# Three quarters of the last down projection as seven half-size block products, with the next quarter's up projection between them

## The chip, the cores and the metric

The kernel runs on one core of one Trainium2 chip, as one program. The time is device microseconds of that core, the median of three runs. A core has TensorE (PE in the rows: matmuls, and PEld: the loads of their stationary operand), VectorE (DVE), ScalarE (ACT), GpSimd (POOL) and SyncE (SP, which issues most of the DMAs). Each engine works through its own instructions in order and waits on semaphores of the others.

## What is computed

A two-layer decoder trunk over 512 tokens of width 1024, all in float32: differential attention and an MLP, then multi-head latent attention and an MLP, then a norm. The change is in the second MLP and in what follows it:

```python
def sq_relu_mlp(hn, w_up, w_down):
    return jnp.square(jax.nn.relu(hn @ w_up)) @ w_down
...
        h = h + sq_relu_mlp(rms_norm(h, mlp_norm_g[l]), w_up[l], w_down[l])
    return rms_norm(h, final_norm_g)
```

Here `hn` is 512 x 1024, `w_up` 1024 x 4096 and `w_down` 4096 x 1024.

## The kernel before

**Three matmuls for one.** Every operand is split into a high part (a cast to the type fp32r, on ScalarE) and a low part (what the cast left over, a subtraction on VectorE). `mm3` multiplies high by high, high by low and low by high, so a float32 product of 128 x 128 by 128 x 512 is three matmuls. Lines 346, 347 and 348 are these three.

**Weights.** The class `Weights` (object `W`) holds a list of units of 128 x 1024 elements in the order in which they are used. A unit is loaded by SP into one of four raw buffers, then cast (L101, `...h`) and subtracted (L113, `...l`) into one of three buffer pairs (`DEPTH`). `W.get` hands out the next unit, `W.ahead` prepares those behind it: as far as one unit ahead. A unit can't be cast before the matmuls of the unit three places earlier have read its buffer.

**The last MLP.** It goes in two halves of the 4096 hidden features. `hidden` makes the up projection: weights stationary, the normed tokens (`xn0`, `xn1`, high and low) moving, two banks of 128 features x 512 tokens at a time from a unit `m1u_0` (inputs 0 to 511) and a unit `m1u_4` (512 to 1023). Each finished bank gets a Relu on ScalarE (L676), a product with itself on VectorE (L677) and a split into high and low (L332, L333), 16 tiles in a half. The first four of these tile pairs go into `krest`, eight 128 x 512 tiles at the low end of SBUF that earlier stages used for attention keys, the others into tiles of the pool `big` (`m1hh`, `m1hl`). `down_tokens` makes the down projection: hidden features stationary (128 features x 128 tokens), weights moving (`m1d_0` to `m1d_14`, eight units of two times 128 features x 512 outputs), four banks of 128 tokens x 512 outputs, once for each half `fc` of the outputs. `token_done` scales a bank by the token's norm factor `r2c` and adds it to the residual tile `rt` on VectorE; behind the second half it also starts the final norm.

A unit is thus 24 matmuls with 512 columns, up or down. The last MLP has 32 units up (16 in each half) and 32 down.

**Beside the first up projection** runs `scale1`: it sums the squares of the stream over features by matmuls (`m1csps`, from `ssq_m`, which GpSimd has added up), makes `r2c`, and turns the residual `res` into token rows by 8 groups of transposes (`rT`), each copied by ScalarE into a tile `rt`. `side` calls the next step of it whenever so many microseconds of matmuls, by the program's own reckoning, have been issued: 4.0.

Nothing but these lists, the buffers and the order in which the code asks for things sets the order; a scheduler in the framework may move instructions of one engine a few places.

Of the kernel before, what the change touches and what calls it, by code (L numbers as in the profile page):

```python
# [15 lines left out]
P = 128  # L16
# [43 lines left out]
class Weights:  # L60
# [5 lines left out]
    def __init__(self, nc, pool, size):  # L66
        self.nc, self.pool, self.size = nc, pool, size
        self.specs, self.raws, self.parts = [], [], []
        self.taken = self.split = 0
        self.eng = nc.vector  # L70
# [13 lines left out]
    def load(self, upto, queue=None):  # L84
        while len(self.raws) < min(upto, len(self.specs)):
            name, shape, loads, *_ = self.specs[len(self.raws)]
            raw = self.tile(F32, name + "r", "raw", shape, self.RAW)
            for to, src in loads:
                (queue or self.nc.sync).dma_start(raw[to], src)
            self.raws.append(raw)  # L90

    def prep_h(self, upto):

        while len(self.parts) < min(upto, len(self.specs)):
            n = len(self.parts)
            self.load(n + 1)
            name, shape, _, beside, outs, eng = self.specs[n]
            h = self.tile(F32R, name + "h", "wh", (P, shape[1], shape[2] * (2 if beside else 1)), self.DEPTH)
            l = h if beside else self.tile(F32R, name + "l", "wl", shape, self.DEPTH)
            for d, v in outs or [(lambda t: t[:, :, :shape[2]], lambda t: t)]:  # L100
                self.nc.scalar.copy(d(h), v(self.raws[n]))  # L101
            self.parts.append((h, l))

    def prep(self, upto):

        self.prep_h(upto)
        while self.split < min(upto, len(self.specs)):
            n = self.split
            name, shape, _, beside, outs, eng = self.specs[n]
# [6 lines left out]
            self.load(n + 1 + self.RAW)  # L116

    def get(self, n):
        assert n == self.taken, (n, self.taken, self.specs[n][0])
# [3 lines left out]
        return got  # L123

    def ahead(self):
        self.prep(self.taken + 1)


class Filler:
# [132 lines left out]
def trunk(ctx: ExitStack, tc: tile.TileContext, io: dict, out: bass.AP):  # L262
# [17 lines left out]
    def bank(name, tag):  # L280
        return ps.tile([P, T], F32, name=name, tag=tag, bufs=BANKS[tag])
# [14 lines left out]
    def w_unit(w, c0, n, k0, nk, name, **kw):  # L296
        return W.add(name, (P, nk, n), [((ALL,), w_view(w, c0, n, k0, nk))], **kw)
# [42 lines left out]
        split_into(h, l, src, scale)  # L340
        return h, l

    def mm3(dst, a, b, start, stop):

        (ah, al), (bh, bl) = a, b
        nc.tensor.matmul(dst, ah, bh, start=start, stop=False)  # L346
        nc.tensor.matmul(dst, ah, bl, start=False, stop=False)  # L347
        nc.tensor.matmul(dst, al, bh, start=False, stop=stop)  # L348
        us = 3 * PASS * max(256, dst.shape[-1])
        later.spent(us)  # L350
        return us
# [451 lines left out]
    last_b = [out_proj(w_ob, heads_b, 4, 4, split_for(xs_m1, G_MLP_B, ssq_m1), "ob", OP_TAGS)]  # L803


    hid1 = [[], []]
# [6 lines left out]
    def down_tokens(w_dn, hid, half, fc, last):  # L813

        units = [(w_unit(w_dn, fc * T, T, 16 * half + k, 2, f"m1d{half}{fc}_{k}"), k) for k in range(0, 16, 2)]
        tags = ("s", "s", "tr", "tr") if (half + fc) % 2 else ("acc", "acc", "acc", "o")
        late = 2 if last else 0

        def job():
            dsts = [bank(f"m1d{half}{fc}{i}", t) for i, t in enumerate(tags)]  # L820

            def mul(i, w, k):
                for kk in range(2):
                    yield mm3(dsts[i], sub(hid[k + kk], ALL, slice(i * P, (i + 1) * P)), sub(w, ALL, kk),
                              k + kk == 0, k + kk == 15)

            for u, k in units[:8 - late]:
                w = W.get(u)
                for i in range(NT):
                    yield from mul(i, w, k)  # L830
                    if i == 1:
                        W.ahead()
                    if k == 14:
                        token_done(i, dsts[i], half, fc)
            ws = [(W.get(u), k) for u, k in units[8 - late:]]
            for i in range(NT if late else 0):
                for w, k in ws:
                    yield from mul(i, w, k)
                token_done(i, dsts[i], half, fc)
        return 16 * NT * 3 * PASS * T, job  # L840

    def token_done(i, dst, half, fc):
        t = rtok[i][fc]
        nc.vector.scalar_tensor_tensor(t, dst, r2c[:, i:i + 1], t, op0=ALU.mult, op1=ALU.add)
        if half == 0:
            return
        junk = big("fjunk")
        nc.scalar.activation(junk, t, AF.Square, accum_out=fss[:, i, fc:fc + 1])
        if fc == 0:
            nc.gpsimd.tensor_mul(t, t, gfin[0][:, :T])  # L850
            nc.vector.tensor_scalar(fss[:, i, 0:1], fss[:, i, 0:1], 1.0 / D, EPS, op0=ALU.mult, op1=ALU.add)
            return
        e, f = small("fe", 1), fr[:, i:i + 1]
        nc.vector.tensor_scalar(e, fss[:, i, 1:2], 1.0 / D, fss[:, i, 0:1], op0=ALU.mult, op1=ALU.add)
        nc.gpsimd.tensor_tensor(f, e, mhalf, op=ALU.pow)

        def out_first():
            o0 = rtok[i][0]
            nc.scalar.activation(o0, o0, AF.Copy, scale=f)
            nc.scalar.dma_start(out_d[i][:, :T], o0)  # L860

        def out_second():
            nc.vector.scalar_tensor_tensor(t, t, f, gfin[0][:, T:], op0=ALU.mult, op1=ALU.mult)
# [4 lines left out]
    up1, down1 = [None, None], [None, None]  # L868
    for half in range(2):
        up1[half] = hidden(io["w_up"][1], xs_m1, half, hid1[half], "m1")  # L870
        down1[half] = [down_tokens(io["w_down"][1], hid1[half], half, fc, half == 1 and fc == 1) for fc in range(2)]


    x_d = io["x"].rearrange("o (i p) d -> (o i) p d", p=P)
# [290 lines left out]
```

## Time and profile before

| | |
|---|---|
| median of 3 runs | 1147.07 us (1147.04 to 1147.47) |
| the profiled execution's own time | 1147.38 us |
| its span, first to last instruction | 1145.6 us |
| TensorE busy | 98% of the span |
| VectorE busy | 57% |
| ScalarE busy | 43% |
| last MLP (start of the first up matmul, of the last down matmul) | 781.46, 1135.72 us |

A row of the timeline has the start in us, the duration, the engine, the line, what it writes and reads, and in brackets how long the engine was idle before it and what ended that. Buffer numbers are left out of names. The duration of a matmul contains its way through the array, so that neighbours overlap; the distance between the starts of two neighbours is what one of them costs. The same holds, less strongly, for VectorE and ScalarE: the next instruction starts somewhat before the end of the one ahead.

### The profile page before, as it was taken

What the parts mean: (1) busy time and instruction counts of PE and PEld (TensorE: products, weight loads), DVE (VectorE), ACT (ScalarE), POOL (GpSimd) and SP (SyncE); (2) the same over time, 40 slices, a digit from 0 to 9 for tenths busy, and PEclk for the clock granted to TensorE, in tenths of its full rate; (3) what the DMA queues carried; (4) which work ended last, traced back from release to release, by engine and by line L of the source; (5) the groups of instructions that cost most, each with busy time, mean ns of one, the idle gap of its engine ahead of it and who ended that gap; (6) DMA issues with size and microseconds to landing.
All of it is one profiled execution on the core that took longest, in us unless ns stands there. A gap on an engine that the chain in (4) does not pass through costs nothing.

```text
span 1145.6 us, 14137 instructions
## 1 busy us (share of the span) xinstructions
PE 1125.5 (98%) x5528; PEld 945.5 (83%) x5528; DVE 649.5 (57%) x1148; ACT 496.9 (43%) x910; POOL 70.6 (6%) x63
## 2 busy tenths in 40 slices
PE   7999999999999999999999999999999999999996
PEld 7778998878888888888888889988888888888885
DVE  5898989876443234444455898855444223444232
ACT  6567666654341213443334666534433112343132
POOL 1000000030000010000111000013000000000011
PEclk9999999999999999999999999999999999999998
DMA  7321222123233333332332220123322333333211
GB/s 230 103 71 56 74 75 75 55 74 111 92 94 108 93 92 93 108 94 92 93 100 80 78 74 19 56 92 92 92 92 92 99 103 92 92 101 101 92 55 74
DMA packets 98321, 102.06 MB, mean 89 GB/s; under 512 B 4896, under 2 KB 86478, under 8 KB 98254
## 3 DMA queue, kind: packets, MB, share of 16 engines
q1 hardware_dynamic: 96974, 99.51, 28.2%
q10 hardware_dynamic: 1280, 1.65, 0.4%
q8 instruction: 43, 0.70, 0.2%
q14 instruction: 24, 0.20, 0.1%
HBM read 99.05 MB, written 2.10 MB: 88 GB/s over the span
## 4 chain that ended last, share of the span: by engine, by line
PE 79%; DVE 12%; ACT 4%; issue 2%; DMA 1%; SPq 1%; POOL 1%; ACTq 0%; POOLq 0%; DVEq 0%
PE m0d L346 5%; PE m1u L346 5%; PE m0d L348 5%; PE m1u L348 5%; PE m0u L347 5%; PE m0u L346 5%; PE m0d L347 5%; PE m1u L347 5%; PE m0u L348 5%; PE m1d L347 4%; PE m1d L348 4%; PE m1d L346 4%; PE m1d L51 3%; PE ob L346 1%; PE ob L348 1%
## 5 line engine op out<-in xcount | busy, mean ns | idle before, releaser
L346 PE MATMUL m1u<-xn1h,m1u_4h 128*128 128x512 f32 x128 | 50.3, 393 | 0.0
L346 PE MATMUL m1u<-xn0h,m1u_0h 128*128 128x512 f32 x128 | 50.2, 392 | 0.0
L348 PE MATMUL m1u<-xn1h,m1u_4l 128*128 128x512 f32 x128 | 49.9, 390 | 0.0
L348 PE MATMUL m1u<-xn0h,m1u_0l 128*128 128x512 f32 x128 | 49.9, 390 | 0.0
L347 PE MATMUL m1u<-xn1l,m1u_4h 128*128 128x512 f32 x128 | 49.8, 389 | 0.0
L347 PE MATMUL m1u<-xn0l,m1u_0h 128*128 128x512 f32 x128 | 49.8, 389 | 0.0
L347 PE MATMUL m0u<-xm0l,m0u_0h 128*128 128x512 f32 x128 | 49.8, 389 | 0.0
L346 PE MATMUL m0u<-xm0h,m0u_0h 128*128 128x512 f32 x128 | 49.8, 389 | 0.0
L346 PE MATMUL m0u<-xm1h,m0u_4h 128*128 128x512 f32 x128 | 49.8, 389 | 0.0
L347 PE MATMUL m0u<-xm1l,m0u_4h 128*128 128x512 f32 x128 | 49.8, 389 | 0.0
L348 PE MATMUL m0u<-xm0h,m0u_0l 128*128 128x512 f32 x128 | 49.8, 389 | 0.0
L348 PE MATMUL m0u<-xm1h,m0u_4l 128*128 128x512 f32 x128 | 49.8, 389 | 0.0
L113 DVE TENSOR_TENSOR m1u_4l<-m1u_4r,m1u_4h 128x1024 fp32r<-128x1024 f32 x16 | 19.6, 1225 | 36.5 <-ACT m1u_4h L101 36.5
L113 DVE TENSOR_TENSOR m0u_4l<-m0u_4r,m0u_4h 128x1024 fp32r<-128x1024 f32 x16 | 19.9, 1245 | 33.4 <-ACT m0u_4h L101 33.2
L677 DVE TENSOR_TENSOR m1a<-m1u,m1a 128x512 f32<-128x512 f32 x32 | 22.0, 687 | 21.7 <-ACT m1a L676 21.7
L677 DVE TENSOR_TENSOR m0a<-m0u,m0a 128x512 f32<-128x512 f32 x32 | 21.9, 686 | 19.4 <-ACT m0a L676 19.4
L101 ACT CAST m1u_4h<-m1u_4r 128x1024 fp32r<-128x1024 f32 x16 | 16.8, 1052 | 34.7 <-PE m1u L347 21.6
L676 ACT ACTIVATE m0a<-m0u 128x512 f32<-128x512 f32 x32 | 18.9, 592 | 29.4 <-PE m0u L348 29.4
L676 ACT ACTIVATE m1a<-m1u 128x512 f32<-128x512 f32 x32 | 19.0, 592 | 27.6 <-PE m1u L348 27.6
L101 ACT CAST m0u_4h<-m0u_4r 128x1024 fp32r<-128x1024 f32 x16 | 16.8, 1052 | 31.7 <-PE m0u L347 25.5
L363 POOL TENSOR_TENSOR ssq_m<-ssq_m,sq 128x512 f32<-128x512 f32 x14 | 21.3, 1519 | 149.8 <-ACT sq L362 149.7
L113 DVE TENSOR_TENSOR m0u_0l<-m0u_0r,m0u_0h 128x1024 fp32r<-128x1024 f32 x16 | 21.0, 1310 | 14.7 <-ACT m0u_0h L101 14.4
(2306 smaller groups left out, 3522.9 us busy)
## 6 DMA issues: line engine op xcount, KB each, us to landing
m0u_0r<-in_w_up SPq DMA_DIRECT2D x16, 512.0 KB, 3.7
m0u_4r<-in_w_up SPq DMA_DIRECT2D x16, 512.0 KB, 3.6
m1u_0r<-in_w_up SPq DMA_DIRECT2D x16, 512.0 KB, 3.6
m1u_4r<-in_w_up SPq DMA_DIRECT2D x16, 512.0 KB, 3.7
wq_0r<-in_w_qkv_a SPq DMA_DIRECT2D x8, 512.0 KB, 3.9
wk_0r<-in_w_qkv_a SPq DMA_DIRECT2D x8, 512.0 KB, 5.0
xt<-in_x SPq DMA_DIRECT2D x8, 256.0 KB, 4.8
wv_0r<-in_w_qkv_a SPq DMA_DIRECT2D x4, 512.0 KB, 3.5
```

What stands on the lines that cost most here:

```text
L51: return self.owner.tc.keep_in_program_order(op(*args, **kw))
L101: self.nc.scalar.copy(d(h), v(self.raws[n]))
L113: eng.tensor_sub(d(to), v(self.raws[n]), d(h).bitcast(F32))
L346: nc.tensor.matmul(dst, ah, bh, start=start, stop=False)
L347: nc.tensor.matmul(dst, ah, bl, start=False, stop=False)
L348: nc.tensor.matmul(dst, al, bh, start=False, stop=stop)
L363: eng(nc).tensor_add(accum, accum, sq)
L676: nc.scalar.activation(a, dst, AF.Relu)
L677: nc.vector.tensor_mul(a, dst, a)
```

## The change

The first three quarters of the hidden features (1024 each, a chunk) get their down projection in another form, the last quarter keeps `down_tokens`. In a chunk the hidden activations A (512 tokens x 1024 features) and the weights B (1024 features x 1024 outputs) are cut in two both ways; A11 is the first 256 tokens and 512 features, B12 the first 512 features and the last 512 outputs. Instead of eight block products there are seven, of blocks and of sums and differences of blocks (S1 to S4 of A, T1 to T4 of B; Winograd's form of Strassen's scheme), and the sums over products are made in three PSUM chains (`u`, `v`, `w`) whose running values are added to `rt` at seven points. A product is 24 matmuls of 512 columns (two units of 12), an eighth of the chunk's old 192.

The hidden activation is now squared by ScalarE (L881 of the new kernel, two pieces of 128 x 256) and kept in float32; the seven left operands are split when they are needed, all into `krest` tiles (a pair of tile pairs per product, in turn). The weights of a chunk are loaded whole: the left column into tiles that attention had used, the right column into `res`, once `scale1` has read it. Weight units may now be such blocks or sums, so `load`, `prep_h` and `prep` skip or call them, and `W.lead = 2` prepares two units ahead while the chunks run. The up projection goes by quarters and by units (`hidden_half`): the first quarter ahead of everything, then one unit of the next quarter behind each product, and one more at a chunk's end. `side` is called with 2.0 in place of 4.0, the norm's weights are two tiles in place of one.

```diff
+            k, ahead = n + 1, 0
+            while k < len(self.specs) and ahead < self.RAW:
+                ahead += not callable(self.specs[k][2])
+                k += 1
+            self.load(k)
...
-        self.prep(self.taken + 1)
+        self.prep(self.taken + self.lead)
...
+        ORDER = (("A11", "B11", "u", [(0, 0)]), ("A12", "B21", "v", [(0, 0)]), ("S2", "T2", "u", [(0, 1)]),
+                 ("S1", "T1", "w", [(1, 1)]), ("S3", "T3", "u", [(1, 1)]), ("S4", "B22", "w", [(0, 1)]),
+                 ("A22", "T4", "u", [(1, 0)]))
...
+        def hidden_tile(self, n, a):
+            k, u, j = n // 4, n % 4 // 2, n % 2
+            for m in range(2):
+                name = f"A{m + 1}{k + 1}"
+                if j == 0:
+                    self.a.setdefault(name, []).append(big(f"m1{name}{self.at}{u}").rearrange("p (k q) -> p k q", k=2))
+                nc.scalar.activation(self.a[name][u][:, j, :], a[:, m * 256:(m + 1) * 256], AF.Square)
...
+        def sum_a(self, to, x, y, op, place=None):
+            x, y = self.a[x], self.a[y]
+            t = self.a[place] if place else [big(f"m1{to}{self.at}{u}").rearrange("p (k q) -> p k q", k=2) for u in range(2)]
+            for u in range(2):
+                nc.vector.tensor_tensor(t[u], x[u], y[u], op)
+            self.a[to] = t
+
+        def sum_b(self, to, x, y, place=None):
+            x, y = self.b[x], self.b[y]
+            t = self.b[place] if place else [[big(f"m1{to}{self.at}{u}{j}") for j in range(2)] for u in range(2)]
+            for u in range(2):
+                if isinstance(t[u], list) or isinstance(x[u], list) or isinstance(y[u], list):
+                    for j in range(2):
+                        nc.vector.tensor_sub(*(v[u][j] if isinstance(v[u], list) else v[u][:, j, :] for v in (t, x, y)))
+                else:
+                    nc.vector.tensor_sub(t[u], x[u], y[u])
+            self.b[to] = t
+
+        def pair(self, name):
+            spare = key_rests[2 * (Sevenths.made % 2):][:2]
+            Sevenths.made += 1
+            self.pairs[name] = [split(a.rearrange("p k q -> p (k q)"), name, tiles=spare[u])
+                                for u, a in enumerate(self.a[name])]
...
+        def product(self, i, units):
+            a, b, chain, to = self.ORDER[i]
+            first = chain not in self.banks
+            if first:
+                self.banks[chain] = [bank(f"m1{chain}{self.at}{t}", "s" if chain == "u" else "tr") for t in range(2)]
+            for u in range(2):
+                w = W.get(units[u])
+                for t in range(2):
+                    for j in range(2):
+                        tok = slice(j * 256 + t * P, j * 256 + (t + 1) * P)
+                        yield mm3(self.banks[chain][t], sub(self.pairs[a][u], ALL, tok), sub(w, ALL, j),
+                                  first and u == j == 0, u == j == 1, skip_group_check=True)
+                        if t == j == 0:
+                            W.ahead()
+                    if u == 1:
+                        for m, n in to:
+                            x = rtok[2 * m + t][n]
+                            tok = 2 * m + t
+                            nc.vector.scalar_tensor_tensor(x, self.banks[chain][t], r2c[:, tok:tok + 1], x,
+                                                           op0=ALU.mult, op1=ALU.add)
...
+        steps = {
+            ("P", 0): lambda: (s.pair("A12"), s.sum_b("T1", "B12", "B11"), s.sum_a("S1", "A21", "A22", ALU.add)),
+            ("U", 0): lambda: (s.sum_b("T2", "B22", "T1"), load("B11")),
+            ("P", 1): lambda: (s.sum_a("S2", "S1", "A11", ALU.subtract), s.pair("S2")),
+            ("U", 1): lambda: s.sum_b("T3", "B22", "B12", "B12"),
+            ("P", 2): lambda: (s.pair("S1"), s.sum_a("S4", "A12", "S2", ALU.subtract, "A12")),
+            ("U", 2): lambda: (s.sum_b("T4", "B21", "T2", "T2"), load("B21")),
+            ("P", 3): lambda: (s.sum_a("S3", "A11", "A21", ALU.subtract, "A21"), s.pair("S3")),
+            ("P", 4): lambda: s.pair("S4"),
+            ("P", 5): lambda: (s.pair("A22"), load("B12")),
+            ("P", 6): lambda: (load("B22"), nxt is not None and nxt.pair("A11")),
+        }
+
+        def with_step(name, gen):
+            for at, us in enumerate(gen):
+                yield us
+                if at == 0 and name in steps:
+                    steps[name]()
+
+        def job():
+            for i in range(7):
+                yield from with_step(("P", i), s.product(i, plan[i]))
+                yield from with_step(("U", i), halves[i]())
+            yield from halves[7]()
+        return (7 * 8 + 8 * 16 / 2) * 3 * PASS * T, job
...
-    side(up1[0], scale1(), 4.0)
-    gfin.append(ap.tile([P, D], F32, name="gfin", tag="atl", bufs=2))
-    nc.sync.dma_start(gfin[0], io["final_norm_g"].rearrange("(o d) -> o d", o=1).broadcast_to([P, D]))
-    Filler(down1[0] + up1[1] + down1[1][:1]).drain()
+    sevenths[0].load_b("B11", "B21")
+    side([(16 * 3 * PASS * T / 2, job) for job in up1[:6]], scale1(), 2.0)
+    sevenths[0].load_b("B12", "B22")
+    sevenths[0].pair("A11")
+    Filler([(16 * 3 * PASS * T / 2, job) for job in up1[6:]]).drain()
+    W.lead = 2
+    Filler(both1).drain()
+    W.lead = 1
+    gfin += [big(f"gfin{n}") for n in range(2)]
+    for n in range(2):
+        nc.sync.dma_start(gfin[n], io["final_norm_g"][n * T:(n + 1) * T].rearrange("(o d) -> o d", o=1).broadcast_to([P, T]))
+    Filler(down1[:1]).drain()
     nc.kept = True
-    Filler(down1[1][1:]).drain()
+    Filler(down1[1:]).drain()
```

Where instructions stand now, at three places. The first is TensorE at the start of the last MLP; `m1u_0_7253` and `m1u_1_7254` (now `..7261`, `..7262`) are the two banks of the first up products, `ssq_m` the sum that GpSimd has made. Before, the 21 matmuls of the first seven `mm3` stood ahead of `m1csps`; these are the rows just around it:

```order
L346 MATMUL m1u_1_7254<-xn0h,m1u_0h 128x512
L347 MATMUL m1u_1_7254<-xn0l,m1u_0h 128x512
L348 MATMUL m1u_1_7254<-xn0h,m1u_0l 128x512
L369 MATMUL m1csps<-ones,ssq_m_7078 128x2 x4
L346 MATMUL m1u_1_7254<-xn0h,m1u_0h 128x512
L347 MATMUL m1u_1_7254<-xn0l,m1u_0h 128x512
```

Now:

```order
L357 MATMUL m1u_0_7261<-xn0h,m1u_0h 128x512
L358 MATMUL m1u_0_7261<-xn0l,m1u_0h 128x512
L359 MATMUL m1u_0_7261<-xn0h,m1u_0l 128x512
L380 MATMUL m1csps<-ones,ssq_m_7078 128x2 x4
L357 MATMUL m1u_1_7262<-xn0h,m1u_0h 128x512
L358 MATMUL m1u_1_7262<-xn0l,m1u_0h 128x512
```

`m1csps` has moved up by nine matmuls: it stands behind the first bank's 12, ahead of the second bank's.

The second place is TensorE in the second chunk, where its first product ends (`m1B1111`, the second unit of block B11, moving, against the split of A11 in `krest`) and the first unit of the up projection woven in begins:

```order
L357 MATMUL m1u_8246<-m1B1111h,krest_73 128x512
L358 MATMUL m1u_8246<-m1B1111l,krest_73 128x512
L359 MATMUL m1u_8246<-m1B1111h,krest_74 128x512
L357 MATMUL m1u_0_8299<-xn0h,m1u_0h 128x512
L358 MATMUL m1u_0_8299<-xn0l,m1u_0h 128x512
L357 MATMUL m1u_1_8300<-xn0h,m1u_0h 128x512
L358 MATMUL m1u_1_8300<-xn0l,m1u_0h 128x512
L359 MATMUL m1u_0_8299<-xn0h,m1u_0l 128x512
```

Nothing stood here before: the up units of a half came in one row, then the down units. The first use of the unit's low part is its fifth matmul.

The third place is VectorE at the same time: behind the sums for T1 come the low part of the left operand's second half, the sums for S1, the low part of that up unit, then the low part of the next product's first weights and the two additions to `rt`:

```order
L908 TENSOR_TENSOR m1T_8257<-res,m1B_7695 128x512
L344 TENSOR_TENSOR krest_70<-m1A_8225,krest_69 128x512
L898 TENSOR_TENSOR m1S_8262<-m1A_7795,m1A_8115 128x512
L898 TENSOR_TENSOR m1S_8263<-m1A_7961,m1A_8227 128x512
L120 TENSOR_TENSOR m1u_0l<-m1u_0r,m1u_0h 128x1024
L120 TENSOR_TENSOR m1B2110l<-m1B_7866,m1B2110h 128x1024
L948 SCALAR_TENSOR_TENSOR rt_7302<-m1u_8245,r2c,rt_7302 128x512
L948 SCALAR_TENSOR_TENSOR rt_7346<-m1u_8246,r2c,rt_7346 128x512
```

In the up projection of before, VectorE had between two such low parts of weights products L677 and low parts L333 of hidden tiles, one of each on average:

```order
L333 TENSOR_TENSOR m1hl<-m1a,m1hh 128x512
L113 TENSOR_TENSOR m1u_0l<-m1u_0r,m1u_0h 128x1024
L677 TENSOR_TENSOR m1a<-m1u_1_7438,m1a 128x512
L333 TENSOR_TENSOR m1hl<-m1a,m1hh 128x512
L113 TENSOR_TENSOR m1u_4l<-m1u_4r,m1u_4h 128x1024
```

In the third chunk the hidden tiles of the last quarter (`m1a`, `m1hl`: still by VectorE) come in between, here in its third product, ahead of the up unit that follows it:

```order
L990 TENSOR_TENSOR m1a<-m1u_0_8917,m1a 128x512
L344 TENSOR_TENSOR krest_72<-m1S_8880,krest_71 128x512
L344 TENSOR_TENSOR krest_74<-m1S_8881,krest_73 128x512
L344 TENSOR_TENSOR m1hl<-m1a,m1hh 128x512
L990 TENSOR_TENSOR m1a<-m1u_1_8918,m1a 128x512
L898 TENSOR_TENSOR m1A_8731<-m1A_8731,m1S_8960 128x512
L898 TENSOR_TENSOR m1A_8843<-m1A_8843,m1S_8961 128x512
L120 TENSOR_TENSOR m1u_0l<-m1u_0r,m1u_0h 128x1024
```

Three of these eight (both L990 and the `m1hl`) are not there in the other two chunks.

## Rows read from the trace of the kernel before

**Rows 1.** The page's head and busy times (share of the span, instructions).

```profile
span 1145.6 us, 14137 instructions
PE 1125.5 (98%) x5528; PEld 945.5 (83%) x5528; DVE 649.5 (57%) x1148; ACT 496.9 (43%) x910; POOL 70.6 (6%) x63
```

**Rows 2.** TensorE's waits: who for whom, total us, times, longest; the longest inside.

```profile
...
PE rb_ps L321 <- POOL r L51: 1.1, 1, 1.1
...
```

**Rows 3.** Windows, up projections of the last MLP: us, busy by engine, clock, DMA.

```profile
781.00:873.00 92.00, 92.00 (x426) 76.13 (x425) 41.09 (x52) 39.62 (x56) 4.10 (x3) 1.00 0.30 93
...
961.00:1051.00 90.00, 90.00 (x398) 74.47 (x397) 42.15 (x49) 35.92 (x48) 0.00 (x0) 1.00 0.30 95
```

**Rows 4.** Timeline of TensorE: first matmuls of neighbouring down units, 24 matmuls each.

```profile
890.11 0.39 PE L346 MATMUL m1d<-m1d_6h,m1hh 128*128 128x512 f32 x1
...
895.55 0.39 PE L346 MATMUL m1d<-m1d_8h,m1hh 128*128 128x512 f32 x1
...
1048.21 0.40 PE L346 MATMUL m1d<-m1d_0h,krest 128*128 128x512 f32 x1
...
1053.81 0.40 PE L346 MATMUL m1d<-m1d_2h,krest 128*128 128x512 f32 x1
```

**Rows 5.** Timeline where the last MLP begins: first up matmul, GpSimd's last sum, `m1csps`.

```profile
781.46 0.39 PE L346 MATMUL m1u<-xn0h,m1u_0h 128*128 128x512 f32 x1
...
783.82 1.78 POOL L363 TENSOR_TENSOR ssq_m<-ssq_m,sq 128x512 f32<-128x512 f32 x1 [1.46 <-ACT sq L362]
...
786.22 0.95 PE L369 MATMUL m1csps<-ones,ssq_m 128*128 128x2 f32 x8
```

**Rows 6.** Timeline of VectorE where it has no pause: neighbours of three kinds.

```profile
536.02 0.75 DVE L336 SCALAR_TENSOR_TENSOR xq0l<-res,gcol,xq0h 128x512 fp32r<-128x512 f32 x1 [0.79 <-ACT xq0h L335]
536.68 0.75 DVE L336 SCALAR_TENSOR_TENSOR xkv0l<-res,gcol,xkv0h 128x512 fp32r<-128x512 f32 x1
...
643.32 0.68 DVE L333 TENSOR_TENSOR krest<-lat,krest 128x512 fp32r<-128x512 f32 x1
643.92 0.68 DVE L333 TENSOR_TENSOR lc1l<-lat,lc1h 128x512 fp32r<-128x512 f32 x1
...
645.67 1.21 DVE L113 TENSOR_TENSOR wukv1l<-wukv1r,wukv1h 128x1024 fp32r<-128x1024 f32 x1
646.80 0.68 DVE L333 TENSOR_TENSOR qn01l<-qn,qn01h 128x512 fp32r<-128x512 f32 x1
```

**Rows 7.** Timeline of ScalarE: casts of 512, 1024 and 512 columns.

```profile
642.83 0.62 ACT L332 CAST lc1h<-lat 128x512 fp32r<-128x512 f32 x1
...
644.09 1.05 ACT L101 CAST wukv1h<-wukv1r 128x1024 fp32r<-128x1024 f32 x1
645.04 0.59 ACT L332 CAST qn01h<-qn 128x512 fp32r<-128x512 f32 x1
```

**Rows 8.** DMA issues of an up unit: KB, median us from issue to landing.

```profile
m1u_0r<-in_w_up SPq DMA_DIRECT2D x16, 512.0 KB, 3.6
```

**Rows 9.** Timeline of TensorE at the program's start, and around a later wait.

```profile
8.05 0.58 PE L51 MATMUL va0vps<-wv_0h,xa0h 128*128 128x256 f32 x1 [1.18 <-ACT wv_0h L51]
...
9.45 0.41 PE L51 MATMUL va0vps<-wv_0h,xa0h 128*128 128x256 f32 x1
9.66 0.41 PE L51 MATMUL va0vps<-wv_0l,xa0h 128*128 128x256 f32 x1
...
13.45 0.28 PE L51 MATMUL va0vps<-wv_4h,xa1l 128*128 128x256 f32 x1
13.57 0.28 PE L51 MATMUL va0vps<-wv_4h,xa1h 128*128 128x256 f32 x1
...
31.61 0.43 PE L321 MATMUL rb_ps<-ident,r 128*128 128x128 f32 x2 [1.05 <-POOL r L51]
...
32.12 0.39 PE L347 MATMUL q<-xa1l,wq_0h 128*128 128x512 f32 x1
32.35 0.39 PE L348 MATMUL q<-xa1h,wq_0l 128*128 128x512 f32 x1
```

More of the change, by code (lines that the diff above doesn't have):

```diff
@@ L96, in prep_h @@
             self.load(n + 1)
-            name, shape, _, beside, outs, eng = self.specs[n]
+            name, shape, loads, beside, outs, eng = self.specs[n]
+            if callable(loads):
+                self.raws[n] = loads()
             h = self.tile(F32R, name + "h", "wh", (P, shape[1], shape[2] * (2 if beside else 1)), self.DEPTH)
@@ L341, in split, with mm3 @@
         return h, l
-    def mm3(dst, a, b, start, stop):
+    def mm3(dst, a, b, start, stop, **kw):
         (ah, al), (bh, bl) = a, b
-        nc.tensor.matmul(dst, ah, bh, start=start, stop=False)
-        nc.tensor.matmul(dst, ah, bl, start=False, stop=False)
-        nc.tensor.matmul(dst, al, bh, start=False, stop=stop)
+        nc.tensor.matmul(dst, ah, bh, start=start, stop=False, **kw)
+        nc.tensor.matmul(dst, ah, bl, start=False, stop=False, **kw)
+        nc.tensor.matmul(dst, al, bh, start=False, stop=stop, **kw)
         us = 3 * PASS * max(256, dst.shape[-1])
@@ L811, in trunk, with down_tokens @@
     out_d = out.rearrange("o (i p) d -> (o i) p d", p=P)
-    def down_tokens(w_dn, hid, half, fc, last):
-        units = [(w_unit(w_dn, fc * T, T, 16 * half + k, 2, f"m1d{half}{fc}_{k}"), k) for k in range(0, 16, 2)]
-        tags = ("s", "s", "tr", "tr") if (half + fc) % 2 else ("acc", "acc", "acc", "o")
+    def down_tokens(w_dn, hid, fc, last):
+        units = [(w_unit(w_dn, fc * T, T, 24 + k, 2, f"m1d{fc}_{k}"), k) for k in range(0, 8, 2)]
+        tags = ("s", "s", "tr", "tr") if fc else ("acc", "acc", "acc", "o")
         late = 2 if last else 0
         def job():
-            dsts = [bank(f"m1d{half}{fc}{i}", t) for i, t in enumerate(tags)]
+            dsts = [bank(f"m1d{fc}{i}", t) for i, t in enumerate(tags)]
             def mul(i, w, k):
@@ L824, in mul @@
                     yield mm3(dsts[i], sub(hid[k + kk], ALL, slice(i * P, (i + 1) * P)), sub(w, ALL, kk),
-                              k + kk == 0, k + kk == 15)
-            for u, k in units[:8 - late]:
+                              k + kk == 0, k + kk == 7)
+            for u, k in units[:4 - late]:
                 w = W.get(u)
@@ L832, in job @@
                         W.ahead()
-                    if k == 14:
-                        token_done(i, dsts[i], half, fc)
-            ws = [(W.get(u), k) for u, k in units[8 - late:]]
+                    if k == 6:
+                        token_done(i, dsts[i], fc)
+            ws = [(W.get(u), k) for u, k in units[4 - late:]]
             for i in range(NT if late else 0):
@@ L866, in token_done, with hidden_half, done @@
         later.add(OUT_US[1], out_second)
[L868 to L871, printed above, removed]
+    CHUNKS = 3
+    sevenths = [Sevenths(c, io["w_down"][1]) for c in range(CHUNKS)]
+    opened = {}
+    def hidden_half(mp, half):
+        def done(m, dst):
+            c, n = mp // 4, 2 * (mp % 4) + m
+            a = big("m1a")
+            nc.scalar.activation(a, dst, AF.Relu)
+            if c < CHUNKS:
+                sevenths[c].hidden_tile(n, a)
+            else:
+                nc.vector.tensor_mul(a, dst, a)
+                hid1.append(split(a, "m1h"))
+        if half == 0:
+            opened[mp] = [None, done]
+        u = w_unit(io["w_up"][1], mp * 256, 256, 4 * half, 4, f"m1u{mp}_{half}")
+        def job():
+            if half == 0:
+                opened[mp][0] = [bank(f"m1u{mp}_{m}", "acc") for m in range(2)]
+            dsts, done = opened[mp]
+            w = W.get(u)
+            for m in range(2):
+                for k in range(4):
+                    yield mm3(dsts[m], sub(w, ALL, k, slice(m * P, (m + 1) * P)), xs_m1[4 * half + k],
+                              half == k == 0, half == 1 and k == 3)
+                    if m == k == 0:
+                        W.ahead()
+                if half == 1:
+                    done(m, dsts[m])
+        return job
@@ new lines, in seven, with load, job @@
+    def seven(c):
+        s, nxt = sevenths[c], sevenths[c + 1] if c + 1 < CHUNKS else None
+        plan, halves = [], []
+        for i in range(7):
+            plan.append(s.plan(i))
+            halves.append(hidden_half(4 * (c + 1) + i // 2, i % 2))
+        halves.append(hidden_half(4 * (c + 1) + 3, 1))
+        def load(*names):
+            if nxt is not None:
+                nxt.load_b(*names)
+        steps = {
[15 more added lines that the diff above has]
+                    steps[name]()
+        def job():
+            for i in range(7):
+                yield from with_step(("P", i), s.product(i, plan[i]))
+                yield from with_step(("U", i), halves[i]())
+            yield from halves[7]()
+        return (7 * 8 + 8 * 16 / 2) * 3 * PASS * T, job
@@ L874, in trunk @@
+    up1 = [hidden_half(mp, h) for mp in range(4) for h in range(2)]
+    both1 = [seven(c) for c in range(CHUNKS)]
+    down1 = [down_tokens(io["w_down"][1], hid1, fc, fc == 1) for fc in range(2)]
     x_d = io["x"].rearrange("o (i p) d -> (o i) p d", p=P)
```

41 lines of the change are left out of this document (32 added, 9 removed).

## The prediction

> **What bounds the kernel now.** I read four views. The busy times come first: TensorE is busy for 1125.5 of 1145.6 us, VectorE for 57% of the span [rows 1]. Then TensorE's waits: this list has eleven entries of 10 us together, none in the last MLP; one of 1.1 us for GpSimd is the third longest [rows 2]. Then the windows: in both up projections of the last MLP TensorE is busy for the whole window at a granted clock of 1.00, VectorE for 41.09 of 92.00 and 42.15 of 90.00 us, ScalarE for 39.62 and 35.92, DMA at 93 and 95 GB/s [rows 3]. So the stage is TensorE's alone, and a matmul taken out is time taken out, as long as VectorE and ScalarE, about half idle, deliver. Last the timeline, for the price of 24 matmuls. Two down units whose stationary operand lies in a `big` tile start 895.55 − 890.11 = 5.44 us apart, two whose stationary operand is in `krest` 1053.81 − 1048.21 = 5.60 [rows 4]. Nothing in those lines is a wait; each krest matmul is 0.007 us longer. The reader should see that the price depends on the place of the stationary tile, since all seven new products read theirs from `krest`.
>
> The profiled execution took 1147.38 us, 0.3 over the median of the runs; sums below start from it and the 0.3 goes off at the end.
>
> **What is removed and added.** Three quarters of the down projection are 24 units of 24 matmuls. `krest` held four of a half's sixteen tile pairs, the first half of a quarter; two halves begin with such a stretch, which is four of their units each (two per `fc`): 8 units at 5.60 and 16 at 5.44, that is 44.8 + 87.0 = 131.8 us. In their place stand 3 × 7 products of 24 matmuls, all with `krest` stationary: 21 × 5.60 = 117.6. The balance is −14.2 us. (72 matmuls are gone; that the change doesn't shorten TensorE's list is thus excluded.) The up units, 32, are the same matmuls as before.
>
> **The earlier `m1csps`.** It stood 21 matmuls behind the start of the up projection and now stands 12 behind. TensorE reaches it at 781.46 + 12 × 5.44 / 24 = 784.18. GpSimd's last sum runs from 783.82 for 1.78, to 785.60 [rows 5]. TensorE's queue is in order, so all up matmuls behind it wait too: 785.60 − 784.18 = 1.42. Before, nothing waited, as 21 matmuls ended behind 785.60 and `m1csps` started at 786.22. Bounds: nothing, if the sum runs much shorter now, and 786.22 − 784.18 = 2.04. I take 1.4, as the sum's inputs don't change. What is late next is nothing: the whole up projection shifts, and its feeders gain.
>
> **Work beside TensorE.** A chunk is 7 products at 5.60 and 8 up units at 5.44: 82.7 us of TensorE. VectorE has there 46 operations of 512 columns (12 for T1 to T4, 8 for S1 to S4 (two each), 14 low parts of left operands, 12 low parts of T1, T2 and T4), 18 of 1024 (8 low parts of up units, 8 of B blocks, 2 for T3) and 14 additions to `rt`. Neighbours without pause start 0.60, 1.13 and 0.66 apart [rows 6], so 27.6 + 20.3 + 9.2 = 57.1 us, 69%; in the third chunk 16 more of 512 for the last quarter's hidden tiles, 66.7 us, 81%. The additions read PSUM and the neighbours measured don't all; their price lies between 0.60 and the duration of 0.75, 1.3 us on a chunk. ScalarE has 16 casts of 1024 (0.95 apart), some 34 of 512 (0.62) and 16 squares of 256 (about half of 0.62): 41 us, 50% [rows 7]. Loads are 16 × 512 KB in 82.7 us, 101 GB/s, near the rate of the windows [rows 3]; one lands in 3.6 us [rows 8], and the blocks of B are issued many products ahead of use. All these cost nothing while TensorE covers them; what counts is whether an engine in order has the next operand in time. Two places are tight.
>
> At a chunk's start the last hidden tile of a quarter appears as ScalarE also casts the first woven up unit (1.05), so Relu, squares and the cast of A11's last part end about 2.8 us behind the last up matmul. VectorE follows with that low part (0.6), two sums of S1 (1.2) and then the up unit's low part (1.2): 5.8. TensorE has the product's 5.60 and four matmuls before that low part is used: 5.60 + 0.9 = 6.5. It is 0.7 early.
>
> In the third chunk's third product, VectorE must do the two extra L990 and the `m1hl` of the order shown. Adding up its queue from the chunk's start, the low part of the next up unit ends at about 27.2 us, needed at 28.1; 0.9 early by the pitches, about 0.1 late by the durations. Everywhere else I find 1.8 us or more. So I put 0.3 us on all stalls, within bounds of 0 (nothing can be gained) and 5 (each of the 3 + 1 tight places late by about a 1024-column operation, 1.2).
>
> **A rule beside the sum.** The Trainium skill, page "TensorE: Matmul & The Clock Gate", section "Step-by-step: what each phase is for", says that the stationary operand has a read port of its own, so that loading it takes no bandwidth from the running matmul. By it the place of that tile would not matter. The trace disagrees: 5.60 against 5.44 [rows 4]. The sum goes by the rows.
>
> **Sum.** 1147.38 − 14.2 + 1.4 + 0.3 = 1134.9 us for a profiled execution; as a median 0.3 less, rounded to 1134.7.
>
> **The rivals.**
>
> *Forecast: 59%, 1133.5 to 1136.5.*
>
> *The krest price isn't tied to the place: 12%.* If the 0.16 us came from what ran beside those units (the first of a down projection, with Relu and splits of the last hidden tiles), the products cost 21 × 5.44 = 114.2, 3.4 less: 1131.3. For it speaks that only first units show it; against, that it is spread over two units evenly, and on later ones in `big` gone [rows 4].
>
> *VectorE or ScalarE is late: 20%.* The hand-made queue leaves 0.7 to 0.9 us at the tight places, and a duration is some 0.1 us more than a pitch [rows 6]. If each tight place and some of the 1.8 us ones are missed, 2 to 6 us of TensorE go: 1137 to 1141. For it speaks that VectorE goes from about 46% [rows 3] to 69 and 81%; against, that a late operation is caught up by the next product, since VectorE has slack over any one chunk.
>
> *The clock falls behind the new wait: 5%.* At the program's start, behind a wait, 256 columns took 9.66 − 9.45 = 0.21 us and later 13.57 − 13.45 = 0.12, which is the lower level of 1.2 GHz and then 2.4; from 8.05 to 13.45 is 5.40 us, half of it lost: 2.7. With it, 1137.4. Against: a 1.05 us wait that ended at 31.61 was followed by 512 columns at 32.35 − 32.12 = 0.23, full pace [rows 9]. The Trainium skill, same page, section "A second HAM failure mode: psum-queue depth-cycling", says that short idles between groups of matmuls can make the clock fall and rise again; the second of these rows doesn't show it, and the granted clock in the windows is 1.00.
>
> *The other side: VectorE becomes the bound: 4%.* The place is the three chunks. VectorE's 57.1 + 57.1 + 66.7 = 180.9 us lie under TensorE's 248.1. To eat the gain of 14.2 − 1.4 − 0.3 = 12.5 us it must need 260.6, 1.44 times the estimate. With 1.6 times, as when sums of two float32 tiles run much slower beside ScalarE and DMA than the subtractions measured, it needs 289, and the kernel takes 1134.7 + 289 − 248 ≈ 1176. Against it stands that subtractions of the same shape keep 0.60 in a busy stretch [rows 6].
>
> **How the numbers follow.** The range holds the forecast, the krest rival below and most late-queue cases and the clock above: 1130.5 (the krest rival with less than the full wait for GpSimd) to 1141. A measurement of this kernel can tell 0.2%, 2.3 us. All cases but the last are faster by more: 0.94; the last is slower: 0.04; between them, a VectorE factor near 1.44, 0.02.
>
> **What would show it.** In the changed kernel's trace: 72 matmuls fewer; products from `krest` at 5.60 a unit (5.44 would be the second rival) and up units still at 5.44; one wait of about 1.4 us by GpSimd's sum at `m1csps`; TensorE waiting nowhere, or by tenths, at the low part of the up unit behind the first product of a chunk and behind the third of the last chunk; VectorE busy for about 70 to 80% in the chunks, more by its durations; the last MLP 12 to 13 us shorter. I am wrong if VectorE's or ScalarE's casts stand as releasers of waits through all products, if an addition to `rt` holds a PSUM bank that a chain is to start in, or if the granted clock leaves 1.00 in the chunks.

## The result, and the profile after

The changed kernel takes 1134.78 us (median of 4 runs, 1134.1 to 1135.8), the kernel before 1147.27 (4 runs): a ratio of 0.9891, interval 0.9879 to 0.9903. The forecast was 1134.7. The total is right to 0.1 us; its terms are not all right, and misses in both directions offset each other, as follows.

The profiled execution of the changed kernel took 1135.29 us, with a span of 1133.5 against 1145.6 [rows 1], 12.1 less. The page's busy times, as in rows 1:

```profile
span 1133.5 us, 14248 instructions
PE 1113.4 (98%) x5456; PEld 933.1 (82%) x5456; DVE 729.4 (64%) x1278; ACT 542.1 (48%) x1012; POOL 70.5 (6%) x63
```

The matmuls are 72 fewer, VectorE is busy for 80 us more, and TensorE's share is the same 98%. TensorE's waits (engine, line, for whom; us, times, longest), first rows of the list:

```profile
PE gps L51 <- DMA grow_attn<-in_attn_norm_g: 4.4, 1, 4.4
PE m1csps L380 <- POOL ssq_m L374: 1.3, 1, 1.3
PE va0vps L51 <- ACT wv_0h L51: 1.2, 1, 1.2
```

The middle one is the only wait in the last MLP. Windows from its start through the three chunks to the last down projection (us, busy of TensorE, its weight loads, VectorE, ScalarE and GpSimd, then granted clock, DMA share, GB/s):

```profile
781.00:832.00 51.00, 49.72 (x232) 40.84 (x231) 16.14 (x20) 24.31 (x42) 3.62 (x3) 0.97 0.33 106
832.40:915.30 82.90, 82.90 (x361) 67.62 (x360) 58.88 (x78) 41.23 (x67) 0.00 (x0) 1.00 0.31 101
915.30:998.20 82.90, 82.90 (x361) 67.63 (x360) 58.88 (x78) 41.23 (x67) 0.00 (x0) 1.00 0.31 100
998.20:1081.10 82.90, 82.90 (x361) 67.63 (x360) 63.10 (x85) 38.63 (x56) 0.00 (x0) 1.00 0.20 64
```

In all three chunks TensorE is busy for the whole window at a clock of 1.00, VectorE for 71%, 71% and 76% (forecast by pitches 69% and 81%; the third window holds 85 operations of VectorE and not the 94 counted, as no later chunk's first sums and low parts fall into it and one hidden tile is finished behind it). The first window is the odd one: the clock is 0.97 there. Finer windows behind the wait (only TensorE's column) show why:

```profile
784.00:786.00 2.00, 0.87 (x8) 1.00 0.69 218
786.00:788.00 2.00, 2.00 (x9) 0.83 0.13 45
788.00:790.00 2.00, 2.00 (x8) 0.50 0.00 0
790.00:792.00 2.00, 2.00 (x9) 0.82 0.00 0
```

Behind the wait at `m1csps` the granted clock fell to 0.50, the level of 1.2 GHz, and came back within some 4 us. That is the rival "the clock falls behind the new wait", given 5%, as a part of what happened. The price of a unit is read from the starts of the first matmuls of the first product, its second half, and the woven up unit and product behind it:

```profile
832.40 0.40 PE L357 MATMUL m1u<-m1B1100h,krest 128*128 128x512 f32 x1
...
838.00 0.39 PE L357 MATMUL m1u<-xn0h,m1u_0h 128*128 128x512 f32 x1
...
843.47 0.40 PE L357 MATMUL m1v<-m1B2100h,krest 128*128 128x512 f32 x1
```

A product is 5.60 us, as the krest units of [rows 4]; an up unit behind it is 5.47, not 5.44.

### The profile page after: what moved, and what is told of

It reads as the page before. It is cut to its first block, busy times and chain, and to the rows that moved or that the text cites. A ratio compares the mean times of both kernels' runs of the same rounds, so it can differ in the third digit from the quotient of the medians.

```text
span 1133.5 us, 14248 instructions
## 1 busy us (share of the span) xinstructions
PE 1113.4 (98%) x5456; PEld 933.1 (82%) x5456; DVE 729.4 (64%) x1278; ACT 542.1 (48%) x1012; POOL 70.5 (6%) x63
## 4 chain that ended last, share of the span: by engine, by line
PE 80%; DVE 11%; ACT 3%; issue 2%; DMA 2%; POOL 1%; SPq 1%; ACTq 0%; POOLq 0%; DVEq 0%
PE m1u L359 7%; PE m1u L357 7%; PE m1u L358 7%; PE m0d L357 5%; PE m0d L359 5%; PE m0u L357 5%; PE m0d L358 5%; PE m0u L358 5%; PE m0u L359 5%; PE ob L357 1%; PE ob L358 1%; PE ob L359 1%; PE m1d L51 1%; PE m1w L357 1%; PE m1w L358 1%
## 5 line engine op out<-in xcount | busy, mean ns | idle before, releaser
L357 PE MATMUL m1u<-xn1h,m1u_1h 128*128 128x512 f32 x128 | 50.3, 393 | 0.0
L359 PE MATMUL m1u<-xn1h,m1u_1l 128*128 128x512 f32 x128 | 50.0, 390 | 0.0
L358 PE MATMUL m1u<-xn1l,m1u_1h 128*128 128x512 f32 x128 | 49.9, 390 | 0.0
L120 DVE TENSOR_TENSOR m1u_0l<-m1u_0r,m1u_0h 128x1024 fp32r<-128x1024 f32 x16 | 19.6, 1223 | 27.0 <-ACT m1u_0h L108 27.0
L120 DVE TENSOR_TENSOR m1u_1l<-m1u_1r,m1u_1h 128x1024 fp32r<-128x1024 f32 x16 | 19.6, 1224 | 23.6 <-ACT m1u_1h L108 23.6
L344 DVE TENSOR_TENSOR krest<-m1A,krest 128x512 fp32r<-128x512 f32 x30 | 20.7, 689 | 21.1 <-ACT krest L343 20.8
L108 ACT CAST m1u_1h<-m1u_1r 128x1024 fp32r<-128x1024 f32 x16 | 16.8, 1052 | 34.0 <-PE m1u L358 23.9
L343 ACT CAST krest<-m1A 128x512 fp32r<-128x512 f32 x30 | 18.4, 617 | 26.1 <-PE m1w L358 11.4
```

The lines of the kernel that those rows point to most:

```text
L343: nc.scalar.copy(h, src)
L344: nc.vector.tensor_sub(l, src, h.bitcast(F32))
L357: nc.tensor.matmul(dst, ah, bh, start=start, stop=False, **kw)
L358: nc.tensor.matmul(dst, ah, bl, start=False, stop=False, **kw)
L359: nc.tensor.matmul(dst, al, bh, start=False, stop=stop, **kw)
```

## The experiments

Times are medians; the kernel before, run beside them, took 1147.0 to 1147.4.

**csps_later**: one step more ahead of `m1csps`.

```diff
     def scale1():
         yield
+        yield
         yield from mlp_scale(ssq_m1[0], r2c, "m1")
```

> One further step ahead in the side task puts m1csps 21 matmuls behind the start again, and every later step two microseconds later. Theory (the wait of 1.3 us causes the fall of the clock behind it): wait and slow matmuls both go, 3.0 us less than the changed kernel's profiled 1135.3, so about 1132.3, and the granted clock stays 1.00 in 781 to 800 us. Rival (the clock falls for another reason, such as the transposes coming in twice as densely): the wait of 1.3 goes, the slow matmuls stay, about 1134.

Measured: 1132.66 us (1132.55 to 1133.1), ratio to before 0.9872, interval 0.9856 to 0.9889. No wait stands in the last MLP, and the clock stays at 1.00 in the same windows:

```profile
784.00:786.00 2.00, 2.00 (x10) 1.00 0.41 110
786.00:788.00 2.00, 2.00 (x14) 1.00 0.44 153
788.00:790.00 2.00, 2.00 (x13) 1.00 0.00 0
```

So wait and fall go together, and the theory holds: with the wait gone, so is the fall. The transposes come in as densely as before (789.3 to 807.2 us, in the changed kernel 788.9 to 807.8), so the rival is out. The four profiled executions without this wait (this one, the kernel before, before_aligned and both) show no fall in the last MLP. From the first up matmul to the last down matmul this kernel took 1122.04 − 781.50 = 340.54 us, the changed one 1124.61 − 780.97 = 343.64: 3.1 less, where 3.0 was expected. The medians differ by 2.1 only. Of the four runs of the changed kernel two have a mean clock of 0.996 (1135.29 and 1135.8) and two 0.997 (1134.1 and 1134.27): the fall seems to come in some executions only, and the profiled one was among them.

**late_low**: the sums of S1 made three times over, ahead of the low part that is needed soonest.

```diff
-            ("P", 0): lambda: (s.pair("A12"), s.sum_b("T1", "B12", "B11"), s.sum_a("S1", "A21", "A22", ALU.add)),
+            ("P", 0): lambda: (s.pair("A12"), s.sum_b("T1", "B12", "B11"), s.sum_a("S1", "A21", "A22", ALU.add),
+                             s.sum_a("S1", "A21", "A22", ALU.add, "S1"), s.sum_a("S1", "A21", "A22", ALU.add, "S1")),
```

> The two sums of S1 are made three times over in every chunk, 4 further operations of 512 columns, 2.4 us, ahead of the up unit's low part on VectorE, which is 0.67 us early in the changed kernel's trace. Theory (slack at this place is 0.67 us and the queue is in order): three waits of about 1.7 us, 5.2 us in all, about 1140; if a wait of this length also makes the clock fall as the one at m1csps did, up to 1.7 more for each, 1145. Rival (VectorE has slack over the chunk, so it is made up before anyone waits): 1134.8.

Measured: 1139.49 us (1138.29 to 1140.09), ratio 0.993, interval 0.9915 to 0.9945; 4.7 more than the changed kernel. The wait stands where it was expected, once in each chunk, at the first use of the low part:

```profile
840.95 0.50 PE L359 MATMUL m1u<-xn0h,m1u_0l 128*128 128x512 f32 x1 [1.16 <-DVE m1u_0l L120]
```

It is 1.16 us and not 1.7, as the framework's scheduler put two matmuls of the next product, 0.46 us, ahead of the waiting one: 2.4 − 0.67 − 0.46 ≈ 1.3. Nothing is made up later within the chunk: the first two such places are 925.31 − 840.95 = 84.36 us apart, the chunks of the changed kernel 915.31 − 832.40 = 82.91, so a wait of 1.16 costs 1.45. The rival is out. The granted clock around all three waits is 1.00.

**later_low**: the same sums four times.

> As the kernel late_low, with the sums of S1 made four times in place of three. There TensorE waited 1.16 us in each chunk at the up unit's low part, and the granted clock stayed 1.00. Now the wait is some 1.2 us longer, 2.4, so 3.6 us more in all: about 1143. Theory (the clock fell at m1csps because eight matmuls of 2 columns follow the wait): clock 1.00 behind these waits, 1143. Rival (the length of the wait decides): the granted clock falls behind each, as at m1csps, some 1.7 us more for each, about 1148.

Measured: 1142.97 us (1142.49 to 1143.47), ratio 0.9964, interval 0.995 to 0.9979. The wait is 2.36 us, three times:

```profile
841.15 0.50 PE L359 MATMUL m1u<-xn0h,m1u_0l 128*128 128x512 f32 x1 [2.36 <-DVE m1u_0l L120]
```

with the clock at 1.00 in every window behind it. So a wait nearly twice as long as the one at `m1csps` made no clock fall here. In this execution the clock did not fall behind the wait of 1.3 at `m1csps` either, whereas in the profiles of five other kernels that have that wait it did. Late_low is thus the sharper comparison: in one and the same execution the clock fell behind the 1.28 us at `m1csps` (0.50 from 788 to 790 us) and not behind the three waits of 1.16.

**unwoven**: the same instructions, products first and up units behind them (the list of the weight units, not shown, is put in the same order).

```diff
...
-                yield from with_step(("P", i), s.product(i, plan[i]))
-                yield from with_step(("U", i), halves[i]())
-            yield from halves[7]()
+                yield from with_step(("P", i), s.product(i, plan[i]))
+                if ("U", i) in steps:
+                    steps["U", i]()
+            for i in range(8):
+                yield from halves[i]()
+                if i == 4 and nxt is not None:
+                    nxt.pair("A11")
```

> The same instructions, but in a chunk all seven products come first and then the eight up units. Theory (the weaving pays for VectorE's work): seven products are 39.2 us of TensorE and hold at least 48.1 us of VectorE's work (46 x 0.60 + 10 x 1.13 + 14 x 0.66), so TensorE waits 9 us or more in each of three chunks: 1162 to 1177 us, slower than the kernel before. Rival (VectorE's mean load of about 70% is what counts, buffers carry the work across): within 3 us of 1134.8.

Measured: 1159.59 us (1159.31 to 1159.86), ratio 1.0106, interval 1.0086 to 1.0126: slower than the kernel before. TensorE's waits in the first chunk's products, and a window of them with all engines:

```profile
PE m1w L358 <- DVE m1T100l L120: 3.3, 1, 3.3
PE m1u L357 <- ACT krest L343: 1.6, 1, 1.6
PE m1u L358 <- DVE m1T300l L120: 0.4, 1, 0.4
```

```profile
840.00:880.00 40.00, 34.72 (x138) 26.15 (x137) 38.75 (x57) 18.49 (x28) 0.00 (x0) 0.96 0.28 89
```

VectorE is busy for 38.75 of 40 us here: it is the bound, as the rival on the other side had it, only not in the woven order. The loss is (1159.6 − 1134.8) / 3 = 8.3 us a chunk, near the 9 expected, but not all of it is waiting: the waits of the first chunk are 3.3 + 1.6 + 0.4 = 5.3 us. Much of the rest is the clock, which the expectation did not hold. In or right behind each of the three waits of 3.3 us it fell to 0.50; in the first chunk finer windows show 0.79 from 853 to 856 us and 0.64 from 856 to 859, by an estimate from these 3 × 0.21 + 3 × 0.36 = 1.7 us at most. In the second and third chunk it is 0.50 from 947 to 950 and from 1037 to 1040. Behind the three waits of 1.6 us it stays at 1.00. Why TensorE waits for less than 9 us was not tried; that the first low parts are made ahead of the products would fit.

**eighth**: an eighth product in each chunk.

```diff
-                 ("A22", "T4", "u", [(1, 0)]))
+                 ("A22", "T4", "u", [(1, 0)]), ("A22", "T4", "w", []))
...
```

> An eighth product in every chunk: A22 and T4 once more, into a bank that nobody reads then, with its casts and low parts, woven ahead of the last up unit. It adds the matmuls that the change took out, in the new order. Theory (TensorE's list decides, the other engines have room): 3 x 5.60 = 16.8 us more, 1151.6, slower than the kernel before. Rival (VectorE is close to the bound, so that its further 4 low parts a chunk and the additions behind them are seen): more than 1154.

Measured: 1152.18 us (1151.32 to 1152.23), ratio 1.0039, interval 1.0023 to 1.0055. That is 17.4 more than with seven, with no wait in the chunks. Two of its three runs are at a mean clock of 0.996, 1152.18 and 1152.23, the third at 0.998, 1151.32, so the medians mix executions with and without the fall at `m1csps`. The two profiled executions both have it: 1150.4 − 1133.5 = 16.9 us of span, 5.6 a product, as expected. The last up unit, which now stands behind a product, has become 5.47, too. With as many matmuls as before, the new order is slower than the old one; all of the gain is the products left out.

**places**: where the stationary and the moving operand lie.

> This kernel leaves out the whole computation: it runs 77 groups of 24 matmuls with 512 columns, in the order of a product (three matmuls per step), each group with its stationary pair at one of 11 places of SBUF and its moving pair at one of 7, on constant data with no other engine at work. Theory of the prediction (the price depends on the place of the stationary tile): groups with the stationary pair at the low places, 0 to 16 KB, take 5.60 us (0.2333 a matmul), those at high places 5.44 (0.2267). Rival (not the place; something else about those units): all groups take the same.

Three neighbours among the groups, with the moving pair 64 KB up and the stationary pair 0, 8 and 16 KB up, at the low end of SBUF, where the krest tiles lie:

```profile
183.61 0.39 PE L82 MATMUL s0m<-room 128*128 128x512 f32 x1
...
189.05 0.39 PE L82 MATMUL s8m<-room 128*128 128x512 f32 x1
...
194.49 0.39 PE L82 MATMUL s16m<-room 128*128 128x512 f32 x1
```

All groups took 5.44 us, but the first, which began at the lower clock (its first matmuls start 0.43 us apart). VectorE still wrote the constant data during the first 48 us; behind that no other engine worked until the output. The prediction's reason for 5.60, the place, falls. The Trainium skill, page "TensorE: Matmul & The Clock Gate", section "Step-by-step: what each phase is for", has the stationary operand on a read port of its own; for places this run agrees, with 5.44 at every one.

**offsets**: whole multiples of 8 KB, as in the last run, keep the two operands at one offset. In the kernel they are not, by the program's layout, which no profile shows: krest begins at 128 modulo 256 bytes, the weights and all large tiles at 64.

> This kernel leaves out the whole computation: 64 groups of 24 matmuls with 512 columns as in a product, on constant data with no other engine at work. Now the stationary pair and the moving pair each start 0 to 256 bytes behind a multiple of 128 bytes. In the changed kernel the krest tiles lie at 0 modulo 128, the weights and all other large tiles at 64. Theory (what costs is that the two operands of a matmul lie at different offsets modulo 128): groups with equal offsets take 5.44 us, those 64 apart 5.60. Rival (not the addresses but what runs beside): all groups take 5.44.

First matmuls of neighbouring groups, the moving pair at an offset of 128 bytes, the stationary pair at 96, 128, 192 and 256:

```profile
266.41 0.40 PE L82 MATMUL s96m<-room 128*128 128x512 f32 x1
272.00 0.39 PE L82 MATMUL s128m<-room 128*128 128x512 f32 x1
277.44 0.40 PE L82 MATMUL s192m<-room 128*128 128x512 f32 x1
283.04 0.39 PE L82 MATMUL s256m<-room 128*128 128x512 f32 x1
```

At equal offsets a group takes 277.44 − 272.00 = 5.44, at others 5.59 and 5.60. Over all groups but the first two, which the start disturbs: equal modulo 256 bytes, 5.44 to 5.48 (with both at 16 bytes, 5.54); different, 5.50 to 5.68, most 5.58 to 5.61, but for two with the stationary pair at 16 (5.44, 5.45). 128 apart is slow as well (5.60), so the "modulo 128" of the expectation was too narrow.

**aligned**: the krest tiles at the weights' offset, by the layout both at 192 modulo 256.

```diff
+    const.tile([P, 16], F32, name="pad0")
     key_rests = [[const.tile([P, T], F32R, name=f"krest{n}{c}") for c in range(2)] for n in range(KEY_RESTS)]
+    const.tile([P, 16], F32, name="pad1")
```

> Two unused constants of 64 bytes, ahead of and behind the krest tiles, put these at 64 modulo 128 like the weights, and move nothing else by other than whole multiples of 128, but the few constants behind. Theory (different offsets): the product units take 5.44 in place of 5.60, 21 x 0.16 = 3.4 us less, and the up units behind them 5.44 in place of 5.47, 0.6 less; with some gain in attention, where krest tiles are used too: 1130 to 1131 us. Rival (what runs beside, or the place as such): 5.60 stays, 1134.8.

Measured: 1130.71 us (1129.32 to 1131.24), ratio 0.9851, interval 0.9835 to 0.9868, 4.1 less than the changed kernel. The same three rows as above:

```profile
832.34 0.39 PE L357 MATMUL m1u<-m1B1100h,krest 128*128 128x512 f32 x1
...
837.78 0.39 PE L357 MATMUL m1u<-xn0h,m1u_0h 128*128 128x512 f32 x1
...
843.22 0.39 PE L357 MATMUL m1v<-m1B2100h,krest 128*128 128x512 f32 x1
```

Product and up unit both take 5.44, with the same matmuls, and the same work beside them: the offset is what costs.

**before_aligned**: the two lines in the kernel before.

> The kernel before with krest tiles at the weights' offset. Theory (the offset costs each matmul that has one operand in krest and the other elsewhere): the 8 down units of the last MLP that use krest as stationary go from 5.60 to 5.44, 1.3 us, with the units behind them 0.1; in the first MLP and in attention, where krest is moving or holds keys, some 50 groups of 6 matmuls are slow by 0.02 to 0.04 us each, about 1 to 2 us: 1144 to 1145 us, so that the change itself, with krest at that offset in both, is worth some 14 us. Rival (only the dense use in the new products costs): 1147.3.

Measured: 1144.8 us (11 runs, 1144.65 to 1145.23), ratio 0.998, interval 0.9971 to 0.9989. The pair of down units that stood 5.60 apart in [rows 4] now stands 1051.90 − 1046.46 = 5.44 apart:

```profile
1046.46 0.39 PE L346 MATMUL m1d<-m1d_0h,krest 128*128 128x512 f32 x1
...
1051.90 0.39 PE L346 MATMUL m1d<-m1d_2h,krest 128*128 128x512 f32 x1
```

So the rival is out: the offset costs in the kernel before, too. With krest at that offset on both sides, the change is worth 1144.8 − 1130.7 = 14.1 us.

**both**: aligned and csps_later together.

> The two edits together: krest tiles at the weights' offset, and m1csps behind 21 matmuls again. Theory (two costs that have nothing to do with each other): the changed kernel's 1134.8 less 4.1 of the one and 2.1 of the other, 1128.6; no wait in the last MLP, all units at 5.44. Rival (the two overlap): 1130 or more.

Measured: 1127.86 us (1127.41 to 1128.27), ratio 0.9832, interval 0.9819 to 0.9846. No wait in the last MLP, products at 5.44, and a gain of 6.9 over the changed kernel, a little more than the two apart. This is the fastest version, and it keeps the whole computation.

## Why the prediction was right, point by point

**What bounds the kernel.** Right: TensorE before and after. An eighth product costs 5.6 us, as much as its matmuls take, and a late low part costs what TensorE waits for it and some 0.3 us more (late_low).

**Removed and added, −14.2.** Right in size for the products: 5.60 each. The reason was wrong: not the place of the stationary tile but its offset from the moving one. The rival "the krest price isn't tied to the place" was right to doubt the place, but expected 5.44, and that price did not come. So the term came out because the new products kept the krest tiles at the old offset. One effect was not in the sum: up units behind a product take 5.47, in all 21 cases, 0.6 us. It could have been read in the trace of the kernel before, where the first unit behind a krest stretch takes 1064.88 − 1059.41 = 5.47:

```profile
1059.41 0.39 PE L346 MATMUL m1d<-m1d_4h,m1hh 128*128 128x512 f32 x1
...
1064.88 0.39 PE L346 MATMUL m1d<-m1d_6h,m1hh 128*128 128x512 f32 x1
```

The three chunks took 1081.1 − 832.4 = 248.7 us where 248.1 had been worked out.

**The wait at `m1csps`, 1.4.** It was 1.28, by GpSimd's sum. What failed is the sentence "What is late next is nothing", and the weight given to the clock rival: in the profiled execution the clock fell behind the wait. The first eight up units with their side work took 832.40 − 780.97 = 51.43 us; before, by the starts in the timeline, 48.42. That is 3.0 more, of which the wait explains 1.3 and the slow matmuls nearly all the rest. csps_later shows that both belong to the wait. The Trainium skill, page "TensorE: Matmul & The Clock Gate", section "A second HAM failure mode: psum-queue depth-cycling", says that frequent short idles between groups of matmuls can make the clock fall and rise. Here a single one, of 1.28 us, was followed by such a fall, and the three of 2.36 us in later_low were not.

**Stalls, 0.3.** None. The two tight places were read correctly: VectorE's low part and its first use at the start of the first chunk, and in the third chunk's third product:

```profile
837.04 1.22 DVE L120 TENSOR_TENSOR m1u_0l<-m1u_0r,m1u_0h 128x1024 fp32r<-128x1024 f32 x1
...
1024.34 1.22 DVE L120 TENSOR_TENSOR m1u_0l<-m1u_0r,m1u_0h 128x1024 fp32r<-128x1024 f32 x1
```

```profile
838.93 0.40 PE L359 MATMUL m1u<-xn0h,m1u_0l 128*128 128x512 f32 x1
...
1026.41 0.40 PE L359 MATMUL m1u<-xn0h,m1u_0l 128*128 128x512 f32 x1
```

The first ends at 838.26 and is used at 838.93: 0.67 early (forecast 0.7). The second ends at 1025.56 and is used at 1026.41: 0.85 (forecast 0.9). Elsewhere the least is 2.15 us (forecast 1.8 or more). late_low confirms the first from the other side.

**Where the total came out.** From the first up matmul to the last down matmul the changed kernel took 1124.61 − 780.97 = 343.64 us, the kernel before 1135.72 − 781.46 = 354.26: 10.6 less, not the 12 to 13 forecast. The 12.1 of the span are completed by two things outside the sum. The last MLP started 0.5 us earlier, of which 0.3 is a shorter wait for a load at the program's start (4.4 in place of 4.7); in csps_later it starts at 781.50, so this is chance. And the span ends 8.9 us behind the last matmul, not 9.9. The latter stands in every profile: 8.8 to 8.9 in the eight with the new form, 9.8 to 9.9 in the two kernels with the old one, though the last store is issued 5.09 us behind the last matmul on both sides. What shortens the end was not tried. So the profiled execution came within 0.4 us of its forecast (1135.29 against 1134.9) because a missed loss of 1.6 and one of 0.6 met a missed gain of 1.0, a chance one of 0.5 and the 0.3 of stalls that did not come. The mechanism and the main term were right; that the total was right to 0.1 us is luck.

**The other rivals.** VectorE as the bound: refuted for the woven order (71 to 76% busy), shown for the unwoven one. VectorE or ScalarE late: did not come, but the distance is 0.67 us, and past it each us is paid for.

## What to carry to other kernels

The slack of the tightest operand can be worked out ahead from pitches and one engine's queue, to 0.1 us, and is a better question than the mean load: VectorE's 71% was free in the woven order, and the same work cost 25 us in the other, in waits and in the slow clock behind them. Where equal matmuls show two prices, look for what differs in their operands and test it alone before naming a cause; here 64 unused bytes on either side of a group of tiles were worth 4.1 us. A wait that is moved onto the busiest engine can cost more than its length, because of what its clock does next.

## What the runs showed of the hardware

- A matmul of 128x128 by 128x512 in fp32r takes 0.2267 us when its stationary and moving operands start at equal offsets modulo 256 bytes, and mostly 0.2325 to 0.2338 when they don't (5.44 against 5.58 to 5.61 per 24), with nothing else running but VectorE's writes of the constant data in the first 48 us. The absolute place made no difference over 160 KB.
- Behind a wait of 1.3 us that ends with eight matmuls of 2 columns, the granted clock fell to 0.50 and was back within some 4 us, in five of six profiled executions. Behind nine waits of 1.16 to 2.36 us that end with matmuls of 512 columns (late_low, later_low, unwoven) it never fell; at the three of 3.3 us in unwoven it fell each time. That the small matmuls made the difference fits this, but they and the wait were not taken apart, and why the fall sometimes stays away is open.
